# First four weight units of a decoder block loaded and multiplied in pairs, with the value banks moved to the other PSUM pool

## The chip, the cores and the metric

The kernel runs on one NeuronCore of one Trainium2 chip. The metric is the device time of one execution in microseconds (us), smaller is better. Before the change the median of three runs is 462.68 us, between 462.61 and 462.75.

## What is computed

One decoder block over 256 positions of width 1024, all in float32. A wide input projection feeds two token mixers: a gated unit over chunks of 128 positions, and attention in which an indexer picks 64 keys for each query. Both are gated, summed and projected, then come a layer norm, a feed-forward part with a causal convolution of width 3, and a second layer norm.

```python
proj = h @ w_in[i]
u, v, q, k, vv, q_idx, k_idx, w_idx, g_a, g_b = jnp.split(proj, SPLIT_POINTS, axis=-1)
...
mix = jax.nn.sigmoid(g_a) * (a_out @ w_branch_a[i]) + jax.nn.sigmoid(g_b) * (b_out @ w_branch_b[i])
y = mix @ w_o[i]
h = layer_norm(ALPHA * h + y, ln1_g[i], ln1_b[i])
...
f = (jax.nn.silu(gate) * val) @ w_down[i]
h = layer_norm(ALPHA * h + f, ln2_g[i], ln2_b[i])
```

The change touches only the first product, `vv`: the attention values, x (256 x 1024) times a 1024 x 1024 slice of `w_in`.

## The kernel before

All weights but a few small ones are laid out by the host as a row of units of 128 x 2048 floats (1024 KB each), in the order in which they are used. Each unit goes through three steps. SyncE (SP) fetches it into a `raw` buffer, of which there are three (`RB = 3`). ScalarE (ACT) rounds it into `hi` (L77), VectorE (DVE) computes the rest into `lo` (L78). A product of two float32 matrices is then made of three matmuls: x-high by w-high, x-low by w-high and x-high by w-low. There are five `hi` and five `lo` buffers. A `raw` buffer may be filled again when both the cast and the subtraction that read it are done.

`take()` hands out the next unit and asks by `prefetch` (L86 to L98) for units up to four ahead. The loads stand in one SP queue, in order: a load that waits for its buffer holds up all loads behind it.

The value product comes first. Its weights are units 0 to 3: units 0 and 1 hold contraction blocks 0 to 3 for output columns 0 to 511 and 512 to 1023, units 2 and 3 hold blocks 4 to 7 for the same two halves of the columns. Within a unit, columns k*512 to k*512+511 belong to one contraction block. x comes transposed, as eight blocks `xt_sb[:, k]` of 128 x 256 (128 KB each), and is split into `xh` and `xl`.

Before the change unit 0 is fetched in four quarters of 256 KB, each followed by one block of x (L152 with L139 and L128), then unit 1 in two halves, then x blocks 4 to 7 in one load (L154), then unit 2 in two halves. Unit 3 comes whole from `prefetch` (L90). The loop L232 to L243 multiplies unit by unit, 24 matmuls of 128 x 512 for each: four blocks by three products by two position tiles `t`. The sums stand in four PSUM banks that are two tiles of pool A (`bankA`, two buffers of two banks each, L230). The ACT copies of L243 take the first column half out after unit 2 and the second after unit 3. The next product, `qi0` (units 4 and 5, `fm_unit`, L183), takes its bank from pool A too, which by then holds both value tiles. Pool B has four single banks.

In the names that the order of the program prints, `raw0` to `raw7`, `hi0`, `lo0` and so on carry the number of the unit, and `vv0` to `vv3` are the value tiles. What follows a last underscore only counts allocations.

Of the kernel before, what the change touches and what calls it, by code (L numbers as in the profile page):

```python
# [9 lines left out]
F32 = mybir.dt.float32  # L10
F32R = mybir.dt.float32r
AF = mybir.ActivationFunctionType
ALU = mybir.AluOpType
AX = mybir.AxisListType

P = 128
# [10 lines left out]
UN = 2048  # L27
# [13 lines left out]
def kernel(  # L41
# [12 lines left out]
    nc = tc.nc  # L54
# [3 lines left out]
    rawp = ctx.enter_context(tc.tile_pool(name="rawp", bufs=RB))  # L58
    hip = ctx.enter_context(tc.tile_pool(name="hip", bufs=HB))
    lop = ctx.enter_context(tc.tile_pool(name="lop", bufs=LB))  # L60
# [5 lines left out]
    def slot(tag, shape, dt=F32, name=None):  # L66
        return slots.tile(shape, dt, tag=tag, name=name or tag)

    def bankA(shape, name):
        return psA.tile(shape, F32, tag="A", name=name)  # L70

    def bankB(shape, name):
        return psB.tile(shape, F32, tag="B", name=name)

    def split(hi, lo, src, scale=None):
        if scale is None:
            a = nc.scalar.copy(hi, src)  # L77
            return a, nc.vector.tensor_tensor(out=lo, in0=src, in1=hi.bitcast(F32), op=ALU.subtract)  # L78
        else:
            nc.scalar.mul(hi, src, scale)  # L80
            nc.vector.scalar_tensor_tensor(lo, src, scale, hi.bitcast(F32), op0=ALU.mult, op1=ALU.subtract)

    units = {}
    state = {"next": 0}

    def prefetch(upto):  # L86
        while state["next"] <= min(upto, wst.shape[0] - 1):
            i = state["next"]
            raw = rawp.tile([P, UN], F32, tag="raw", name=f"raw{i}")
            nc.sync.dma_start(out=raw, in_=wst[i])  # L90
            hi = hip.tile([P, UN], F32R, tag="hi", name=f"hi{i}")
            lo = lop.tile([P, UN], F32R, tag="lo", name=f"lo{i}")
            n = 4 if i < 4 else 2
            for c in range(n):
                cs = slice(c * UN // n, (c + 1) * UN // n)
                split(hi[:, cs], lo[:, cs], raw[:, cs])
            units[i] = (hi, lo)
            state["next"] += 1  # L98
# [3 lines left out]
    def take(ahead=AHEAD):  # L102
        i = cur["i"]
        cur["i"] += 1
        prefetch(i + ahead)
        return units[i]
# [16 lines left out]
    xt_sb = slot("b2", [P, 2, KC, L], name="xt_sb")[:, 0]  # L123
    x2 = slot("x2", [P, 2, KC, L], F32R, name="x2")
    xh, xl = x2[:, 0], x2[:, 1]

    def load_x(a, b):
        nc.sync.dma_start(out=xt_sb[:, a:b], in_=xt[:, a:b])  # L128

    def load_unit(pieces, pre=None):  # L130
        i = state["next"]
        state["next"] += 1
        raw = rawp.tile([P, UN], F32, tag="raw", name=f"raw{i}")
        hi = hip.tile([P, UN], F32R, tag="hi", name=f"hi{i}")
        lo = lop.tile([P, UN], F32R, tag="lo", name=f"lo{i}")
        n = UN // pieces
        for c in range(pieces):
            cs = slice(c * n, (c + 1) * n)
            nc.sync.dma_start(out=raw[:, cs], in_=wst[i][:, cs])  # L139
            if pre:  # L140
                pre(c)
                with tc.issue_after(prev.ins) if c else nullcontext():
                    nc.vector.tensor_copy(xh[:, c:c + 1], xt_sb[:, c:c + 1])  # L143
                nc.vector.tensor_tensor(out=xl[:, c:c + 1], in0=xt_sb[:, c:c + 1], in1=xh[:, c:c + 1].bitcast(F32),
                                        op=ALU.subtract)
            m = max(1, n // 512)
            for d in range(m):
                ds_ = slice(c * n + d * n // m, c * n + (d + 1) * n // m)
                prev = split(hi[:, ds_], lo[:, ds_], raw[:, ds_])[1]
        units[i] = (hi, lo)  # L150

    load_unit(4, lambda c: load_x(c, c + 1))  # L152
    load_unit(2)
    load_x(4, 8)  # L154
    split(xh[:, 4:8], xl[:, 4:8], xt_sb[:, 4:8])
    load_unit(2)

    ident = const.tile([P, P], F32, name="ident")
    make_identity(nc, ident)
# [23 lines left out]
    def fm_unit(name, m2, hook=None):  # L183
        hi, lo = take()
        bank = bankA([P, 2, 2, L], name)
        fm_chunks(hi, lo, m2, bank, hook)
        return bank

    def fold(bank, dst=None, name="fold"):
        if dst is None:  # L190
            dst = work.tile([P, 2, L], F32, tag="w", name=name)
        nc.scalar.copy(dst, bank[:, :, 1, :])  # L192
        nc.vector.tensor_tensor(out=dst, in0=bank[:, :, 0, :], in1=dst, op=ALU.add)  # L193
        return dst
# [32 lines left out]
            nc.vector.tensor_tensor(out=qs[b, hs, :], in0=bank[a], in1=qs[a, hs, :].bitcast(F32), op=ALU.subtract)  # L227

    vv = a2a[:, 0].rearrange("p (t d) -> p t d", d=D)
    vpair = [bankA([P, 2, 512], f"vv{t}") for t in range(2)]  # L230
    vbanks = [vpair[i // 2][:, i % 2] for i in range(4)]
    for kh in range(2):  # L232
        for hf in range(2):
            hi, lo = take()
            for k in range(4):
                for n, (a, b) in enumerate(((xh, hi), (xl, hi), (xh, lo))):
                    kk = 4 * kh + k
                    for t in range(2):
                        nc.tensor.matmul(vbanks[2 * t + hf], a[:, kk, t * P:(t + 1) * P], b[:, k * 512:k * 512 + 512],  # L239
                                         start=kk == 0 and n == 0, stop=kk == KC - 1 and n == 2)  # L240
            if kh == 1:
                for t in range(2):
                    nc.scalar.copy(vv[:, t, hf * 512:(hf + 1) * 512], vbanks[2 * t + hf])  # L243

    wkb = slot("k", [P, 2, KC, 72], F32R, name="wkb")
    wkh = wkb[:, 0]
# [6 lines left out]
    for u in range(2):  # L253
        b = fold(fm_unit(f"qi{u}", x2), name=f"qif{u}")
# [64 lines left out]
    for u in range(4):  # L319
        b = fm_unit(f"q{u}", x2, {0: kidx_norm, 2: kidx_transpose}.get(u))  # L320
# [6 lines left out]
    for u in range(4):  # L327
        b = fm_unit(f"k{u}", x2)
# [48 lines left out]
    for g, dst in ((0, ga), (1, gb)):  # L377
        for u in range(4):
            i = 4 * g + u
# [4 lines left out]
            b = fm_unit(f"g{g}{u}", x2)  # L384
# [58 lines left out]
    for u in range(4):  # L443
        b = fold(fm_unit(f"u{u}", x2), name=f"uf{u}")
# [7 lines left out]
    for u in range(4):  # L452
        b = fold(fm_unit(f"wb{u}", b2), name=f"wbf{u}")
# [7 lines left out]
    for u in range(4):  # L461
        b = fold(fm_unit(f"wa{u}", a2), name=f"waf{u}")
# [169 lines left out]
    for t in range(2):  # L632
# [25 lines left out]
        for c0, eng in ((512, nc.scalar), (768, nc.sync)):  # L658
            cs = slice(c0, c0 + 256)
# [72 lines left out]
```

## Time and profile before

| | |
|---|---|
| median of three runs | 462.68 us |
| the profiled execution | 463.17 us |
| its span in the profile | 461.5 us |
| TensorE (PE) busy | 450.4 us, 98% of the span |
| DVE, ACT busy | 353.2 us (77%), 258.9 us (56%) |
| moved by DMA | 86.83 MB, 188 GB/s in the mean |

The profile shows one execution. Times within it are counted from the start of the span, and 1.7 us of the execution lie outside of the span. A busy matmul includes its time in the pipeline (about 0.39 us for a 128 x 512 one), so the pace of the engine is read from the distance between starts. A row of a timeline merges neighbouring instructions of one kind; in brackets stands how long the engine idled before it and what ended the wait.

### The profile page before, as it was taken

What the parts mean: (1) busy time and instruction counts of PE and PEld (TensorE: products, weight loads), DVE (VectorE), ACT (ScalarE), POOL (GpSimd) and SP (SyncE); (2) the same over time, 40 slices, a digit from 0 to 9 for tenths busy, and PEclk for the clock granted to TensorE, in tenths of its full rate; (3) what the DMA queues carried; (4) which work ended last, traced back from release to release, by engine and by line L of the source; (5) the groups of instructions that cost most, each with busy time, mean ns of one, the idle gap of its engine ahead of it and who ended that gap; (6) DMA issues with size and microseconds to landing.
All of it is one profiled execution on the core that took longest, in us unless ns stands there. A gap on an engine that the chain in (4) does not pass through costs nothing.

```text
span 461.5 us, 6329 instructions
## 1 busy us (share of the span) xinstructions
PE 450.4 (98%) x2470; PEld 385.4 (84%) x2470; DVE 353.2 (77%) x582; ACT 258.9 (56%) x381; POOL 8.2 (2%) x19
## 2 busy tenths in 40 slices
PE   7999999999999999999999999999999999999993
PEld 3778888888888888898888899888888888888883
DVE  4768878977776559688686869999878677777746
ACT  3678645456474548555454238977655655655600
POOL 0000002000000100001000000000000000000000
PEclk9999999999999999999999999999999999999998
DMA  7978646445344644547746128655654554552002
GB/s 233 381 272 309 260 181 227 178 188 182 104 171 141 254 167 168 190 178 250 297 182 223 51 92 287 241 197 188 240 216 171 194 183 183 182 183 91 2 0 91
DMA packets 14989, 86.83 MB, mean 188 GB/s; under 512 B 1648, under 2 KB 2928, under 8 KB 5744
## 3 DMA queue, kind: packets, MB, share of 16 engines
q1 hardware_dynamic: 13536, 81.98, 48.5%
q0 software_dynamic: 1136, 4.19, 2.7%
q8 instruction: 19, 0.31, 0.3%
q10 hardware_dynamic: 288, 0.26, 0.2%
q14 instruction: 10, 0.08, 0.0%
HBM read 85.39 MB, written 1.05 MB: 187 GB/s over the span
## 4 chain that ended last, share of the span: by engine, by line
PE 95%; DMA 1%; DVE 1%; SPq 1%; ACT 0%; issue 0%; DVEq 0%; ACTq 0%
PE up L171 16%; PE up L170 8%; PE g L171 6%; PE dn L110 4%; PE dn L111 4%; PE dn L109 4%; PE vv L239 4%; PE g L170 3%; PE k L171 3%; PE u L171 3%; PE q L171 3%; PE wb L171 3%; PE wa L171 3%; PE wa L170 2%; PE wb L170 2%; PE q L170 2%
## 5 line engine op out<-in xcount | busy, mean ns | idle before, releaser
L78 DVE TENSOR_TENSOR lo<-raw,hi 128x1024 fp32r<-128x1024 f32 (+1 forms) x158 | 181.0, 1164 | 20.1 <-ACT hi L77 20.0
L77 ACT CAST hi<-raw 128x1024 fp32r<-128x1024 f32 (+1 forms) x158 | 154.5, 1007 | 30.5 <-PE dn L111 12.7
L171 PE MATMUL up<-h,hi 128*128 128x512 f32 x320 | 113.2, 398 | 0.0
L170 PE MATMUL up<-h,lo 128*128 128x256 f32 x320 | 90.0, 281 | 0.0
L171 PEld LDWEIGHTS up<-h,hi 128*128 128x128 f32 x320 | 60.1, 188 | 14.6
L170 PEld LDWEIGHTS up<-h,lo 128*128 128x128 f32 x320 | 60.4, 189 | 0.3
L171 PE MATMUL g<-x,hi 128*128 128x512 f32 x128 | 45.0, 393 | 0.0
L170 PE MATMUL g<-x,lo 128*128 128x256 f32 x128 | 36.5, 286 | 0.0
L193 DVE TENSOR_TENSOR upf<-up,upf 128x512 f32<-128x512 f32 x20 | 13.8, 690 | 19.6 <-ACT upf L192 19.6
L171 PEld LDWEIGHTS g<-x,hi 128*128 128x128 f32 x128 | 24.0, 187 | 5.2
L192 ACT COPY upf<-up 128x512 f32<-128x512 f32 x20 | 11.7, 584 | 27.5 <-PE up L171 27.5
L170 PEld LDWEIGHTS g<-x,lo 128*128 128x128 f32 x128 | 24.2, 189 | 0.0
L532 ACT ACTIVATE y<-upf,cv_sb 128x256 f32<-128x256 f32 x40 | 21.9, 595 | 2.8 <-DVE upf L193 2.8
L171 PE MATMUL u<-x,hi 128*128 128x512 f32 x64 | 22.7, 399 | 0.0
L171 PE MATMUL k<-x,hi 128*128 128x512 f32 x64 | 22.7, 399 | 0.0
L171 PE MATMUL q<-x,hi 128*128 128x512 f32 x64 | 22.5, 393 | 0.0
L171 PE MATMUL wb<-b,hi 128*128 128x512 f32 x64 | 22.3, 391 | 0.0
L171 PE MATMUL wa<-a,hi 128*128 128x512 f32 x64 | 22.2, 391 | 0.0
L239 PE MATMUL vv<-hi,x 128*128 128x512 f32 x64 | 18.6, 402 | 2.2 <-DVE x L143 0.7
L533 DVE SCALAR_TENSOR_TENSOR y<-upf,cv_sb,y 128x255 f32<-128x255 f32 x40 | 17.7, 479 | 0.7 <-ACT y L532 0.7
L170 PE MATMUL wb<-b,lo 128*128 128x256 f32 x64 | 18.2, 284 | 0.0
L170 PE MATMUL q<-x,lo 128*128 128x256 f32 x64 | 18.1, 282 | 0.0
(222 smaller groups left out, 888.1 us busy)
## 6 DMA issues: line engine op xcount, KB each, us to landing
raw<-in_wst_dram SPq DMA_DIRECT2D x72, 1024.0 KB, 4.9
raw<-in_wst_dram SPq DMA_DIRECT2D x4, 512.0 KB, 8.9
raw<-in_wst_dram SPq DMA_DIRECT2D x4, 256.0 KB, 4.3
a2a<-in_par_dram POOLq DMA_DIRECT2D x2, 512.0 KB, 4.7
l1p<-in_par_dram POOLq DMA_DIRECT2D x2, 512.0 KB, 8.5
hres<-in_x_dram POOLq DMA_DIRECT2D x1, 1024.0 KB, 5.1
xt_sb<-in_xt_dram SPq DMA_DIRECT2D x4, 128.0 KB, 4.2
xt_sb<-in_xt_dram SPq DMA_DIRECT2D x1, 512.0 KB, 9.1
```

Of the source, the lines that this page charges most:

```text
L77: a = nc.scalar.copy(hi, src)
L78: return a, nc.vector.tensor_tensor(out=lo, in0=src, in1=hi.bitcast(F32), op=ALU.subtract)
L109: nc.tensor.matmul(ps, ah, bh, start=start, stop=False)
L110: nc.tensor.matmul(ps, ah, bl, start=False, stop=False)
L111: nc.tensor.matmul(ps, al, bh, start=False, stop=stop)
L170: nc.tensor.matmul(ps[:, 0, :], wl, m2k[:, 0], start=start, stop=False, skip_group_check=True)
L171: nc.tensor.matmul(ps, wh, m2k, start=False, stop=stop, skip_group_check=True)
L192: nc.scalar.copy(dst, bank[:, :, 1, :])
L193: nc.vector.tensor_tensor(out=dst, in0=bank[:, :, 0, :], in1=dst, op=ALU.add)
L239: nc.tensor.matmul(vbanks[2 * t + hf], a[:, kk, t * P:(t + 1) * P], b[:, k * 512:k * 512 + 512], start=kk == 0 and n == 0, stop=kk == KC - ...
L532: nc.scalar.activation(y[:, c, :], b[:, c, :], AF.Identity, scale=cv_sb[:, 2, ch:ch + 1], bias=cv_sb[:, 3, ch:ch + 1])
L533: nc.vector.scalar_tensor_tensor(y[:, c, 1:], b[:, c, :L - 1], cv_sb[:, 1, ch:ch + 1], y[:, c, 1:], op0=ALU.mult, op1=ALU.add)
```

## The change

The first four units are loaded as two pairs by a new `load_units`. For units 0 and 1 each of four steps fetches one block of x, then the quarter of unit 0 and the quarter of unit 1 that go with it. For units 2 and 3 each of two steps fetches two blocks of x and a half of each unit. The splits of x are all on DVE now, and the splits of the weights are made to stand behind them. The value loop goes by contraction blocks over both units of a pair (12 matmuls for a block), keeps its four sums in the single banks of pool B, and copies all four out at its end.

```diff
+    def split_x(a, b, after=None):
+        with tc.issue_after(after.ins) if after else nullcontext():
+            nc.vector.tensor_copy(xh[:, a:b], xt_sb[:, a:b])
+        return nc.vector.tensor_tensor(out=xl[:, a:b], in0=xt_sb[:, a:b], in1=xh[:, a:b].bitcast(F32), op=ALU.subtract)
+
+    def load_units(x0, pieces):
+        pair = []
+        for i in (state["next"], state["next"] + 1):
...
+            units[i] = (hi, lo)
+            pair.append((i, raw, hi, lo))
+        state["next"] += 2
+        n, xn = UN // pieces, 4 // pieces
+        prev = None
         for c in range(pieces):
...
+            load_x(x0 + c * xn, x0 + (c + 1) * xn)
+            for i, raw, hi, lo in pair:
+                cs = slice(c * n, (c + 1) * n)
+                nc.sync.dma_start(out=raw[:, cs], in_=wst[i][:, cs])
+            xs = split_x(x0 + c * xn, x0 + (c + 1) * xn, prev)
+            with tc.issue_after(xs.ins):
+                for d in range(n // 512):
+                    for i, raw, hi, lo in pair:
+                        ds_ = slice(c * n + d * 512, c * n + (d + 1) * 512)
+                        prev = split(hi[:, ds_], lo[:, ds_], raw[:, ds_])[1]
+
+    load_units(0, 4)
+    load_units(4, 2)
...
-    vpair = [bankA([P, 2, 512], f"vv{t}") for t in range(2)]
-    vbanks = [vpair[i // 2][:, i % 2] for i in range(4)]
+    vbanks = [bankB([P, 512], f"vv{i}") for i in range(4)]
     for kh in range(2):
...
+        pair = [take() for _ in range(2)]
+        for k in range(4):
+            kk = 4 * kh + k
+            for n, (a, part) in enumerate(((xh, 0), (xl, 0), (xh, 1))):
+                for hf in range(2):
                     for t in range(2):
...
+                        nc.tensor.matmul(vbanks[2 * hf + t], a[:, kk, t * P:(t + 1) * P], pair[hf][part][:, k * 512:k * 512 + 512],
                                          start=kk == 0 and n == 0, stop=kk == KC - 1 and n == 2)
...
+    for hf in range(2):
+        for t in range(2):
+            nc.scalar.copy(vv[:, t, hf * 512:(hf + 1) * 512], vbanks[2 * hf + t])
```

The queue of loads on SP, from the fourth quarter of unit 0 to the load of unit 4, stands before the change as

```order
L139 DMA raw0_93<-in_wst_dram 128x512
L128 DMA xt_sb_91<-in_xt_dram 128x256
L139 DMA raw1_120<-in_wst_dram 128x1024 x2
L128 DMA xt_sb_91<-in_xt_dram 128x1024
L139 DMA raw2_136<-in_wst_dram 128x1024 x2
L90 DMA raw3_161<-in_wst_dram 128x2048
L90 DMA raw4_173<-in_wst_dram 128x2048
```

and from the third quarters of units 0 and 1 to the load of unit 4 after it as

```order
L150 DMA raw0_93<-in_wst_dram 128x512
L150 DMA raw1_96<-in_wst_dram 128x512
L128 DMA xt_sb_91<-in_xt_dram 128x256
L150 DMA raw0_93<-in_wst_dram 128x512
L150 DMA raw1_96<-in_wst_dram 128x512
L128 DMA xt_sb_91<-in_xt_dram 128x512
L150 DMA raw2_135<-in_wst_dram 128x1024
L128 DMA xt_sb_91<-in_xt_dram 128x512
L150 DMA raw3_138<-in_wst_dram 128x1024
L150 DMA raw2_135<-in_wst_dram 128x1024
L150 DMA raw3_138<-in_wst_dram 128x1024
L90 DMA raw4_181<-in_wst_dram 128x2048
```

Units 0 and 1 now arrive together, quarter by quarter. The first load of unit 3, which fills the buffer of unit 0, stands ahead of the second half of unit 2 and of unit 4.

On PE the first contraction block of the value product stands before the change as the first rows of

```order
L239 MATMUL vv0_159<-hi0_94,x2_92 128x512
L239 MATMUL vv1_160<-hi0_94,x2_92 128x512
L239 MATMUL vv0_159<-hi0_94,x2_92 128x512
L239 MATMUL vv1_160<-hi0_94,x2_92 128x512
L239 MATMUL vv0_159<-lo0_95,x2_92 128x512
L239 MATMUL vv1_160<-lo0_95,x2_92 128x512
```

and after it as

```order
L241 MATMUL vv0_177<-hi0_94,x2_92 128x512
L241 MATMUL vv1_178<-hi0_94,x2_92 128x512
L241 MATMUL vv0_177<-hi0_94,x2_92 128x512
L241 MATMUL vv2_179<-hi1_97,x2_92 128x512
L241 MATMUL vv3_180<-hi1_97,x2_92 128x512
L241 MATMUL vv1_178<-hi0_94,x2_92 128x512
L241 MATMUL vv2_179<-hi1_97,x2_92 128x512
L241 MATMUL vv3_180<-hi1_97,x2_92 128x512
L241 MATMUL vv0_177<-lo0_95,x2_92 128x512
L241 MATMUL vv1_178<-lo0_95,x2_92 128x512
L241 MATMUL vv2_179<-lo1_98,x2_92 128x512
L241 MATMUL vv3_180<-lo1_98,x2_92 128x512
```

A block has 12 matmuls in place of 6, and needs a quarter of two units in place of one.

On DVE the work of the first two blocks stands after the change as

```order
L132 CAST x2_92<-xt_sb_91 128x256
L133 TENSOR_TENSOR x2_92<-xt_sb_91,x2_92 128x256
L78 TENSOR_TENSOR lo0_95<-raw0_93,hi0_94 128x512
L78 TENSOR_TENSOR lo1_98<-raw1_96,hi1_97 128x512
L132 CAST x2_92<-xt_sb_91 128x256
L133 TENSOR_TENSOR x2_92<-xt_sb_91,x2_92 128x256
L78 TENSOR_TENSOR lo0_95<-raw0_93,hi0_94 128x512
```

Before it a block had one subtraction of weights (`lo0`); now a block has two, and the split of the next block of x stands behind both.

## Rows read from the trace of the kernel before

**Rows 1.** Page, first part: busy time of each engine.
```profile
PE 450.4 (98%) x2470; PEld 385.4 (84%) x2470; DVE 353.2 (77%) x582; ACT 258.9 (56%) x381; POOL 8.2 (2%) x19
```

**Rows 2.** Windows: stretch, length, busy time by engine, PE clock, DMA share, GB/s.
```profile
31.00:61.00 30.00, 30.00 (x175) 25.95 (x176) 25.11 (x41) 21.51 (x29) 0.00 (x0) 1.00 0.80 300
...
271.00:301.00 30.00, 29.71 (x195) 26.93 (x195) 26.35 (x37) 25.71 (x35) 0.00 (x0) 1.00 0.58 211
...
421.00:451.00 30.00, 30.00 (x152) 25.41 (x151) 18.48 (x32) 10.39 (x15) 0.00 (x0) 1.00 0.01 3
```

**Rows 3.** Chain that ended last, 0 to 80 us: start, length, what.
```profile
4.08 6.69 DMA xt_sb<-in_xt_dram
...
24.63 5.54 PE vv L239 x23
```

**Rows 4.** Timeline of PE, value product and start of qi0: start, length, instructions.
```profile
4.98 1.24 PE L239 MATMUL vv<-hi,x 128*128 128x512 f32 x4 [0.56 <-ACT hi L77]
...
14.50 1.07 PE L239 MATMUL vv<-hi,x 128*128 128x512 f32 x4
...
22.66 1.07 PE L239 MATMUL vv<-hi,x 128*128 128x512 f32 x4
...
30.83 0.38 PE L170 MATMUL qi<-x,lo 128*128 128x256 f32 x1 [0.45 <-ACT a2a L243]
```

**Rows 5.** Waits of PE, 5 to 31 us: total, times, longest.
```profile
PE vv L239 <- ACT a2a L243: 0.5, 1, 0.5
PE qi L170 <- ACT a2a L243: 0.5, 1, 0.5
```

**Rows 6.** Timeline of ACT, casts that a landing released.
```profile
4.25 0.62 ACT L77 CAST hi<-raw 128x512 fp32r<-128x512 f32 x1 [2.16 <-DMA raw<-in_wst_dram]
5.48 0.62 ACT L77 CAST hi<-raw 128x512 fp32r<-128x512 f32 x1 [0.62 <-DMA raw<-in_wst_dram]
7.60 0.62 ACT L77 CAST hi<-raw 128x512 fp32r<-128x512 f32 x1 [1.50 <-DMA raw<-in_wst_dram]
9.85 0.62 ACT L77 CAST hi<-raw 128x512 fp32r<-128x512 f32 x1 [1.63 <-DMA raw<-in_wst_dram]
12.05 2.41 ACT L77 CAST hi<-raw 128x512 fp32r<-128x512 f32 x4 [1.58 <-DMA raw<-in_wst_dram]
...
15.88 2.41 ACT L77 CAST hi<-raw 128x512 fp32r<-128x512 f32 x4 [0.23 <-DMA raw<-in_wst_dram]
```

**Rows 7.** Timeline of DVE: the split of an x block, the subtractions of unit 0.
```profile
4.54 0.29 DVE L143 CAST x<-xt_sb 128x256 fp32r<-128x256 f32 x1 [4.54 <-DMA xt_sb<-in_xt_dram]
4.87 0.43 DVE L144 TENSOR_TENSOR x<-xt_sb,x 128x256 fp32r<-128x256 f32 x1
5.21 0.69 DVE L78 TENSOR_TENSOR lo<-raw,hi 128x512 fp32r<-128x512 f32 x1
...
11.00 0.68 DVE L78 TENSOR_TENSOR lo<-raw,hi 128x512 fp32r<-128x512 f32 x1
```

**Rows 8.** Timeline of SP's queue: first load, load of unit 3.
```profile
0.81 0.38 SPq L139 DMA_DIRECT2D raw<-in_wst_dram  x1
...
11.71 0.33 SPq L90 DMA_DIRECT2D raw<-in_wst_dram  x1
```

**Rows 9.** Waits of SP's queue, 0 to 35 us: total, times, longest.
```profile
SPq L90 <- DVE lo L78: 14.9, 5, 5.2
```

**Rows 10.** Windows of the loading stage, columns as in rows 2.
```profile
7.00:9.00 2.00, 1.94 (x7) 0.97 (x6) 1.20 (x4) 0.62 (x1) 0.00 (x0) 1.00 0.67 191
...
13.00:15.00 2.00, 2.00 (x11) 1.62 (x10) 2.00 (x4) 1.74 (x4) 0.00 (x0) 1.00 1.05 432
```

**Rows 11.** Page, DMA issues: KB each, median us from issue to landing.
```profile
raw<-in_wst_dram SPq DMA_DIRECT2D x72, 1024.0 KB, 4.9
...
raw<-in_wst_dram SPq DMA_DIRECT2D x4, 256.0 KB, 4.3
```

More of the change, by code (lines that the diff above doesn't have):

```diff
@@ L128, in load_x @@
         nc.sync.dma_start(out=xt_sb[:, a:b], in_=xt[:, a:b])
[L130 to L136, printed above, removed]
-        for c in range(pieces):
[L138 to L156, printed above, removed]
+    def split_x(a, b, after=None):
[5 more added lines that the diff above has]
+        for i in (state["next"], state["next"] + 1):
+            raw = rawp.tile([P, UN], F32, tag="raw", name=f"raw{i}")
+            hi = hip.tile([P, UN], F32R, tag="hi", name=f"hi{i}")
+            lo = lop.tile([P, UN], F32R, tag="lo", name=f"lo{i}")
+            units[i] = (hi, lo)
[3 more added lines that the diff above has]
+        prev = None
+        for c in range(pieces):
+            load_x(x0 + c * xn, x0 + (c + 1) * xn)
[8 more added lines that the diff above has]
+                        prev = split(hi[:, ds_], lo[:, ds_], raw[:, ds_])[1]
@@ L229 @@
     vv = a2a[:, 0].rearrange("p (t d) -> p t d", d=D)
-    vpair = [bankA([P, 2, 512], f"vv{t}") for t in range(2)]
-    vbanks = [vpair[i // 2][:, i % 2] for i in range(4)]
+    vbanks = [bankB([P, 512], f"vv{i}") for i in range(4)]
     for kh in range(2):
[L233 to L237, printed above, removed]
+        pair = [take() for _ in range(2)]
[3 more added lines that the diff above has]
+                for hf in range(2):
                     for t in range(2):
-                        nc.tensor.matmul(vbanks[2 * t + hf], a[:, kk, t * P:(t + 1) * P], b[:, k * 512:k * 512 + 512],
+                        nc.tensor.matmul(vbanks[2 * hf + t], a[:, kk, t * P:(t + 1) * P], pair[hf][part][:, k * 512:k * 512 + 512],
                                          start=kk == 0 and n == 0, stop=kk == KC - 1 and n == 2)
-            if kh == 1:
-                for t in range(2):
-                    nc.scalar.copy(vv[:, t, hf * 512:(hf + 1) * 512], vbanks[2 * t + hf])
+    for hf in range(2):
+        for t in range(2):
+            nc.scalar.copy(vv[:, t, hf * 512:(hf + 1) * 512], vbanks[2 * hf + t])
     wkb = slot("k", [P, 2, KC, 72], F32R, name="wkb")
```

## The prediction

> **What bounds the kernel now.** I read the busy shares first: PE is at work for 450.4 of 461.5 us [rows 1]. The windows then show where the rest lies. From 31 to 451 us PE is busy throughout: of 14 stretches of 30 us one shows 29.71, the others at least 29.99 [rows 2], where the first, that one and the last stand. What the change can give or take therefore shows at one point, the start of `qi0` at 30.83 us [rows 4]; whatever moves this start moves the end by as much, so long as later units still come in time.
>
> Next the timeline of PE up to this point. In steady flow six value matmuls start every 1.36 us: the rows at 14.50 and 22.66 are six such groups apart, 8.16 us for 36 matmuls, so 0.227 us each [rows 4]. All 96 need 21.8 us. They take 25.85 (4.98 to 30.83), so PE loses 4.1 us, in three places:
>
> - The group that starts at 22.66 should end at 24.02, and the next unit starts at 24.63 [rows 3, 4]: 0.6 us. Unit 3 writes the second halves of the same PSUM tiles whose first halves are being copied out; the wait is on that copy [rows 5].
> - Unit 3's 24 matmuls need 5.44 us from 24.63, and `qi0` starts 6.20 later: 0.8 us, on the last copies, since both tiles of pool A are taken [rows 5].
> - The other 2.7 us lie before 12 us. There the chain is a load of x [rows 3]: PE eats a block in 1.36 us, and a block plus its quarter (384 KB) comes every 2.2 us (casts released at 5.48, 7.60, 9.85) [rows 6].
>
> **What the change does to each.** *Banks.* The four sums get tiles of their own, and pool A is free for `qi0`. Both bank waits go: 1.4 us. The copies now stand on ACT behind the casts of units 4 and 5, which costs nothing as far as I can see: the next user of these banks comes some 11 us of matmuls later.
>
> *Pairs.* A block now brings 640 KB for 12 matmuls (2.72 us) in place of 384 KB for 6 (1.36 us). Bytes per matmul fall from 64 to 53 KB. When the bytes have come in order, the old rows tell: 256 KB were there at 4.25, 384 at 4.54, 640 at 5.48, 1024 at 7.60, 1408 at 9.85, 2048 at 12.05, 3584 at 15.88 [rows 6, 7]. I lay the new order on this curve. The x block and the quarter of unit 0 (384 KB) are there at 4.54, and after a cast of 0.62 and the 0.11 that a matmul starts behind it (4.25 + 0.62 to 4.98) PE begins at 5.3, against 4.98. Unit 1's quarter comes 0.94 later and costs about half a microsecond. Block 0 ends at 8.4. Block 1 waits for 1280 KB (9.1, cast until 9.8) and ends at 12.1; block 2 needs 1920 KB (11.6) and ends at 14.7; block 3 ends at 17.5. Half of the product is then done, and the other half would end at 28.4, if its data were there: 2.4 us earlier than now.
>
> *The third buffer.* They are not all there. `raw` has three buffers, and unit 3 takes that of unit 0. Before, unit 0 was finished alone, at 11.68, and unit 3 was issued at 11.71 [rows 7, 8]; it was needed after 72 matmuls. Now unit 0 is finished with block 3 only, and unit 3 is needed in block 4, after 50. SP does wait for this release before the change too: five waits on DVE's `lo`, 14.9 us in all [rows 9]. When is unit 0 released? DVE goes through a block as split of x (0.29 and 0.43), `lo` of unit 0, `lo` of unit 1 (0.69 each) [rows 7], in order. For block 2 `lo` of unit 1 follows 1920 KB at 11.6 plus a cast of 0.62, so 13.0; then block 3's split and `lo` of unit 0, 1.41: 14.4. So the first half of unit 3 is issued at about 14.45. No row has 512 KB alone from an idle queue. Below stand 256 KB, 3.4 us from issue to cast (0.81 to 4.25) [rows 6, 8]; above a whole unit, median 4.9 [rows 11]. I take 4.1, the middle, and keep both ends. It lands at 18.55, is cast at 19.17, and PE, which had done two matmuls of block 4 by 17.95, stands for 1.3 us until 19.3. The other 46 matmuls take 10.4: `qi0` starts at 29.7, not 30.83.
>
> The second half of unit 2 is queued behind the waiting load. It is needed after 22 further matmuls, at 24.3, and follows the half of unit 3 by about 1.3 us at the rate of full flow (432 GB/s) [rows 10], so it lands near 20. Unit 4 follows at about 24 and is needed at 29.7. Units 5 to 7 shift by up to 3 us with some 2 us to spare. I cost these at nothing; if unit 5 slips, `qi1` waits.
>
> For the fixed part of a load, the Trainium skill (DMA: Bandwidth & Descriptors, Anatomy of one DMA) fits about 2.0 us plus bytes at 436 GB/s on another issuing path. By that 512 KB would take an estimated 3.2 us in place of my 4.1 and `qi0` would start 0.9 us earlier; the 256 KB row, at 3.4 against 2.6 by the fit, says that the fit is short here.
>
> *Sum.* `qi0` at 29.7 against 30.83: 1.1 us off. On the profiled execution 463.17 becomes 462.1; this execution lies 0.49 above the median of the runs, so on the median I forecast 462.68 - 1.1 = **461.6 us**. The same in other terms: 1.4 from the banks and 2.7 from the starving go; back come 0.3 of later start, 1.3 for the third buffer and 1.4 that remain of waiting in the first three blocks.
>
> **Bounds.** The unknown terms are the pace of the small loads and the landing of unit 3. From 256 KB at 4.25 to 1408 KB at 9.85 the old kernel took in 211 GB/s, and full flow is 432 [rows 6, 10].
>
> **Rivals.**
>
> - *Small loads run faster.* If the slow pace belongs to the first microseconds alone, or to the many short loads of x, which are now a smaller share, quarters may come at 350 GB/s or more. PE then starts at 5.3 and waits 0.5 only; unit 0 is released at about 12, and unit 3 lands by 16.1, in time. `qi0` starts at 5.3 + 0.5 + 21.8 = 27.6: 3.2 off, 459.5 us. For it speaks that the rate was 432 as soon as the pieces were larger. Against it, 191 GB/s were moved from 7 to 9 us, with much already issued [rows 10].
> - *The third buffer takes the gain back.* With unit 3 landing after 4.9 us in place of 4.1, `qi0` starts at 30.5: 0.3 off, 462.4, which no measurement can tell from no change. A measurement of this kernel tells about 0.2%, 0.93 us.
> - *Slower: the small pace stays for all twelve pieces, and unit 3 pays for it.* At 211 GB/s the last quarter of unit 0 (2304 KB) comes at 14.2, `lo` is done at 15.7, and unit 3, with 4.9 us to land, is there at 20.6. PE waits until 21.3, `qi0` starts at 31.8, 0.9 to 1.0 later: 463.6. It decides at a landing of 19.7: behind this the kernel is slower. The Trainium skill speaks for this one (DMA: Bandwidth & Descriptors, Bandwidth): loads should be batched to a mebibyte or more. The change goes the other way, from eight short loads at the start to twelve, and no run here yet shows the pace of such a longer row.
>
> **How the numbers follow.** I give the forecast 0.43, the fast pace 0.20, the gain taken back 0.27, the slow one 0.10. The forecast lies only 0.2 us beyond what can be told, so a fifth of its chance goes to no change. Faster by over 0.2%: 0.34 + 0.20 = 0.54; same: 0.09 + 0.27 = 0.36; slower: 0.10. The range reaches from near the fast case to short of the slow one's worst: 459.7 to 463.4. The likeliest value is 461.6.
>
> **What would show it.** In the profile after, the waits of PE on the copies of `vv` ahead of `qi0` are gone. `qi0` starts at 29.7. SP issues the first half of unit 3 near 14.4, released by DVE's `lo`, and PE waits once for more than a microsecond early in block 4, for ACT's cast of unit 3. From then on PE is without gaps as before. I am wrong if that issue comes at 12 or 16, if unit 3's half lands outside 17.8 to 19.4, or if a gap shows behind `qi0`, at `qi1` or `kwb`, because units 5 or 6 slipped.

## The result and the profile after

| | median | from | to | executions |
|---|---|---|---|---|
| before | 462.86 us | 462.21 | 463.76 | 12 |
| after | 465.17 us | 463.62 | 468.13 | 12 |

The ratio is 1.0054, with a 95% interval of 1.0037 to 1.0072. The kernel became slower by half a per cent; forecast were 461.6 us and a range of 459.7 to 463.4. The profiled execution, 463.62 us, is the fastest of the twelve, so its profile shows the change at its best.

The page of the kernel after, busy shares and DMA issues [rows 1, 11]:

```profile
PE 450.5 (98%) x2470; PEld 387.2 (84%) x2470; DVE 354.0 (77%) x585; ACT 258.0 (56%) x380; POOL 8.2 (2%) x19
...
raw<-in_wst_dram SPq DMA_DIRECT2D x8, 256.0 KB, 6.2
raw<-in_wst_dram SPq DMA_DIRECT2D x4, 512.0 KB, 5.1
```

The busy shares are those of before. The windows of the kernel after [rows 2, 10]:

```profile
7.00:9.00 2.00, 2.00 (x6) 1.61 (x5) 0.51 (x2) 0.33 (x1) 0.00 (x0) 1.00 1.01 359
...
31.00:61.00 30.00, 28.36 (x165) 24.21 (x164) 26.75 (x43) 23.61 (x33) 0.00 (x0) 1.00 0.79 297
```

Before, PE was busy throughout from 31 to 61 us. Now 1.64 us are missing there. The timeline of PE after [rows 4] shows what was won and where it went:

```profile
5.53 3.71 PE L241 MATMUL vv<-hi,x 128*128 128x512 f32 x8 [1.12 <-ACT hi L77]
...
10.00 1.98 PE L241 MATMUL vv<-hi,x 128*128 128x512 f32 x8
...
18.17 2.02 PE L241 MATMUL vv<-hi,x 128*128 128x512 f32 x8
...
29.11 0.28 PE L173 MATMUL qi<-x,lo 128*128 128x256 f32 x1
...
49.59 0.32 PE L269 MATMUL kwp<-ident,a2a 72*128 72x72 f32 x2 [1.64 <-DVE a2a L263]
```

`qi0` starts 1.7 us earlier, at 29.11 in place of 30.83. The two transposes `kwp` then stand at 49.59, after a wait; without it they would follow the matmul at 47.55 by 0.23. They read the folded product `kwb` (L262, L263). This product is made of x and of `wk`, a small load of its own, and comes behind `qi1` on PE. (`fm_unit` takes one unit: `qi0` is the product of unit 4 alone, not of units 4 and 5, and `qi1` that of unit 5.) Units 6 to 9 stand before its fold only through the order of work on ACT and DVE: the matmuls of `kwb` ended at 43.4, and its copy (L262) came up on ACT at 46.98, behind the casts of units 8 and 9. The waits of PE up to 70 us [rows 5]; the waits on the copies of `vv` are gone:

```profile
PE kwp L269 <- DVE a2a L263: 1.6, 1, 1.6
PE vv L241 <- ACT hi L77: 1.1, 1, 1.1
```

In the trace of before the subtractions of unit 2, the same fold and `kwp` stand so:

```profile
16.82 2.49 DVE L78 TENSOR_TENSOR lo<-raw,hi 128x512 fp32r<-128x512 f32 x4
...
48.08 0.42 DVE L261 TENSOR_TENSOR a2a<-kwb,a2a 72x256 f32<-72x256 f32 x1
...
49.06 0.29 PE L267 MATMUL kwp<-ident,a2a 72*128 72x72 f32 x2
```

The fold ended at 48.50, and PE came to `kwp` at 49.06: the room was 0.56 us, not 2. After the change PE comes at 47.78 (1.28 earlier, one pair of matmuls of the lead having moved ahead of `kwp` in PE's order) and the fold ends at 49.46 (0.96 later). Less the room that makes 1.68; `kwp` starts 0.13 behind the fold, and the sum is the 1.81 us from 47.78 to 49.59, of which the profile counts 1.64 as idle. The chain that ended last, kernel after [rows 3], tells why the fold is late:

```profile
13.87 3.88 DMA raw<-in_wst_dram
17.77 0.63 ACT hi L77
...
21.30 0.69 DVE lo L78
22.01 7.37 DMA raw<-in_wst_dram
29.49 2.00 ACT hi L77 x2
31.48 0.43 ACT a2a L245
...
32.34 0.60 ACT a2a L245
32.94 0.96 ACT hi L77
...
39.33 0.61 DVE qif L196
39.97 0.62 ACT qs L229
...
41.25 1.06 ACT hi L77
...
49.03 0.43 DVE a2a L263
49.59 0.32 PE kwp L269 x2
```

Read from the top: the first half of unit 3 is issued at 13.87, when the buffer of unit 0 is free, and lands 3.88 later. The second half of unit 2 stands behind it in SP's queue and lands at 18.98, 1.9 later than before; on DVE it then stands behind the first half of unit 3 and a split of x. So unit 2 is subtracted (`lo`, 21.30) late; its buffer goes to unit 5, asked for at 22.01 in place of 19.34 and cast at 29.49. (This load took 7.4 us in both traces.) The copies of `vv` (`a2a` L245) and the cast of unit 6 follow that cast on ACT, and each next step stands behind the last, down to the fold. Before, the subtractions of unit 2 ended at 19.31, and the casts of units 4 and 5 ran in one row on ACT from 24.95:

```profile
24.95 3.93 ACT L77 CAST hi<-raw 128x1024 fp32r<-128x1024 f32 x4
...
31.15 2.02 ACT L77 CAST hi<-raw 128x1024 fp32r<-128x1024 f32 x2
...
40.31 2.00 ACT L77 CAST hi<-raw 128x1024 fp32r<-128x1024 f32 x2
```

Unit 6 was cast at 31.15 (32.82 after) and unit 8 at 40.31 (41.25 after). SP's waits after [rows 9] name the hold itself:

```profile
SPq L90 <- DVE lo L78: 6.9, 3, 3.2
...
SPq L150 <- DVE lo L78: 1.8, 1, 1.8
```

### The profile page after: what moved, and what is told of

Its sections match the earlier page's. It is cut to its first block, busy times and chain, and to the rows that moved or that the text cites. A ratio compares the mean times of both kernels' runs of the same rounds, so it can differ in the third digit from the quotient of the medians.

```text
span 461.9 us, 6337 instructions
## 1 busy us (share of the span) xinstructions
PE 450.5 (98%) x2470; PEld 387.2 (84%) x2470; DVE 354.0 (77%) x585; ACT 258.0 (56%) x380; POOL 8.2 (2%) x19
## 4 chain that ended last, share of the span: by engine, by line
PE 87%; DVE 4%; DMA 4%; ACT 2%; issue 1%; SPq 1%; DVEq 0%; ACTq 0%
PE up L174 16%; PE up L173 8%; PE g L174 6%; PE dn L110 4%; PE dn L111 4%; PE dn L109 4%; DMA raw<-in_wst_dram 4%; PE g L173 3%; PE u L174 3%; PE k L174 3%; PE wb L174 3%; PE wa L174 3%; DVE lo L78 3%; PE q L174 3%; PE wa L173 2%; PE wb L173 2%
## 5 line engine op out<-in xcount | busy, mean ns | idle before, releaser
L241 PE MATMUL vv<-hi,x 128*128 128x512 f32 x64 | 17.6, 421 | 1.1 <-ACT hi L77 1.1
```

Of the source, the lines that this page charges most:

```text
L241: nc.tensor.matmul(vbanks[2 * hf + t], a[:, kk, t * P:(t + 1) * P], pair[hf][part][:, k * 512:k * 512 + 512], start=kk == 0 and n == 0, st ...
```

## The experiments

"Traced" is the profiled execution. `qi0` is its start, "rest" the span less that start: what everything behind the value product took. "Wait" is what PE stood at `kwp` or `kT2ps` (the transposes of the indexer keys, later on), "clock" the granted clock from 46 to 61 us where it was not full. Ratios are to runs of the kernel before on the same chip.

| kernel | median (n) | ratio, interval | `qi0` | wait | clock | rest |
|---|---|---|---|---|---|---|
| before | 462.86 (12) | | 30.83 | none | | 430.7 |
| after | 465.17 (12) | 1.0054, 1.0037 to 1.0072 | 29.11 | 1.6 | | 432.8 |
| same_again | 467.77 (1) | | 29.61 | 3.8 | 0.89 | 436.5 |
| late_hook | 466.88 (9) | 1.0076, 1.0053 to 1.0098 | 29.32 | 0.4 + 2.7 | 0.72 (60 to 66) | 436.4 |
| warm11 | 466.44 (7) | 1.0046, 1.0008 to 1.0084 | 29.19 | 3.9 | 0.77 | 437.4 |
| banks_only | 462.37 (10) | 0.9970, 0.9958 to 0.9982 | 29.47 | 0.2 | | 430.7 |
| banks_again | 462.13 (10) | 0.9972, 0.9962 to 0.9983 | 29.23 | 0.2 | | 430.8 |
| first_pair | 462.35 (10) | 0.9967, 0.9945 to 0.9988 | 29.68 | none | | 431.0 |
| own_buffer | 461.83 (10) | 0.9961, 0.9943 to 0.9980 | 28.45 | 2.2 | 0.89 | 434.5 |
| own_again | 462.25 (12) | 0.9972, 0.9961 to 0.9983 | 28.66 | 1.2 | | 432.4 |
| unit2_first | 462.72 (12) | 0.9985, 0.9973 to 0.9997 | 29.07 | 1.5 | | 432.7 |
| u8_late | 463.02 (10) | 0.9984, 0.9967 to 1.0000 | 28.71 | 0.7 | | 431.9 |
| own_u8_late | 462.70 (10) | 0.9970, 0.9950 to 0.9990 | 29.50 | 0.8 | | 431.9 |
| banks_u8_late | 462.67 (10) | 0.9982, 0.9967 to 0.9997 | 29.36 | 0.7 | | 431.2 |
| own_two | 461.91 (6) | 0.9965, 0.9952 to 0.9979 | 29.54 | none | | 430.6 |

The last column is the study in short. Where PE waits by 0.2 us or less behind `qi0`, the rest takes 430.6 to 431.0 us, whatever the loads look like. Where it waits longer, the rest grows by the wait and by what the clock loses (read from the distance between starts: 1.4 us in same_again and own_buffer, 1.7 in late_hook, 2.7 in warm11), to within a microsecond.

**The kernel after once more** (unchanged, one execution).

> The changed kernel once more, nothing edited. Chain theory (what was gained before qi0 is lost in one wait of PE at the transposes kwp near 48 us, because the casts and subtractions of units 5 to 7 come later): again 463.6 us, within 0.3. Clock theory (in most executions PE's clock is at its lower level for some microseconds of the first 30 us, and that makes the spread from 463.6 to 468.1): a time above 464, a mean granted clock below 0.996, and in the trace value matmuls that start 0.43 us apart, in place of 0.227, in a stretch outside of that seen in the first profile (5.5 to 9.1 us).

Measured 467.77. The waits of PE, the windows, and on ACT the cast of unit 8:

```profile
PE kwp L269 <- DVE a2a L263: 3.8, 1, 3.8
```

```profile
46.00:61.00 15.00, 11.17 (x58) 9.47 (x57) 12.84 (x25) 10.53 (x15) 0.00 (x0) 0.89 0.70 258
```

```profile
43.94 2.00 ACT L77 CAST hi<-raw 128x1024 fp32r<-128x1024 f32 x2 [2.24 <-DMA raw<-in_wst_dram]
```

A slower execution of the same kernel waits 2.2 us longer at the same place, since unit 8 lands late: it took 7.1 us from its issue, 4.8 in the first trace. From the end of the wait on the granted clock is lower: from `kwp` to the sixth matmul of `q` with `lo` PE takes 3.30 us, 1.94 in the first trace, so 1.4 us are lost. Against before: 1.2 won at `qi0`, 5.8 lost behind it. The clock theory of the expectation, a slow stretch in the first 30 us, is not what made this execution long; the clock fell at 51.8. The other eleven executions of the kernel after were not traced, but their mean granted clocks fit the same picture: the six above 465 us show 0.990 to 0.993, five of the six below it 0.995 to 0.998 (463.81 has 0.991).

**`kwp` later in PE's order.**

```diff
...
-        b = fm_unit(f"q{u}", x2, {0: kidx_norm, 2: kidx_transpose}.get(u))
+        b = fm_unit(f"q{u}", x2, {1: kidx_norm, 2: kidx_transpose}.get(u), (0, 3) if u == 1 else (0, 5))
```

> The changed kernel with the transposes kwp put 12 matmuls later in PE's order (from the first product q0 into q1). Chain theory: the wait of 1.6 to 1.9 us at kwp goes, and no other takes its place; the median falls by about 1.7, to 463.5 from 465.2, and an execution with the clock of the first profile takes 461.9. Clock theory alone: the spread of some 4 us stays, and the median stays within 0.5 of 465.2. Both: median near 463.5 with the spread.

The waits of PE in late_hook:

```profile
PE kT2ps L287 <- DVE a2a L282: 2.7, 2, 2.1
...
PE kwp L269 <- DVE a2a L263: 0.4, 1, 0.4
```

On ACT, the cast of unit 9:

```profile
45.18 2.00 ACT L77 CAST hi<-raw 128x1024 fp32r<-128x1024 f32 x2 [2.57 <-DMA raw<-in_wst_dram]
```

It failed, 466.88: the transposes moved back by 12 matmuls only, and the next user of the same chain, `kT2ps`, then waits 2.7. The lateness is in the data, not in the place of the instruction that reads it. Its source in this execution is another: unit 5 landed 5.2 us after its issue, and units 5 to 8 were cast as early as before (27.15, 30.48, 34.09, 40.13). Unit 9 took 7.5 us and was cast 2.5 us later than before (42.72).

**A longer warm-up of PE** (`WARM = 8` becomes 11).

> The changed kernel with 11 warm-up matmuls in place of 8, so that PE is at work until about 5.7 us and no gap lies ahead of the first value matmul at 5.5. Clock theory: value matmuls start 0.227 us apart from their first on, the mean granted clock is 0.997 in every execution, and the spread goes: all times between 463.2 and 464.0, since the wait at kwp stays and takes what the front gains. Chain theory alone, with the spread from elsewhere (the loads): median near 465.2 with times up to 468.

The wait of PE behind the product in warm11:

```profile
PE kwp L269 <- DVE a2a L263: 3.9, 1, 3.9
```

466.44, still slower than before. The value product's waits fell to 0.5 us, and the wait at `kwp` was 3.9, with unit 8 landing 7.1 us after its issue. The slow first block of the product is not the cause of the loss.

**The banks alone** (to the kernel before).

```diff
-    vpair = [bankA([P, 2, 512], f"vv{t}") for t in range(2)]
-    vbanks = [vpair[i // 2][:, i % 2] for i in range(4)]
+    vbanks = [bankB([P, 512], f"vv{i}") for i in range(4)]
```

> The kernel before with one part of the change: the value sums in four single banks of pool B; loads and order of the matmuls as before. qi0 starts about 1.4 us earlier, at 29.4. Chain theory: before the change kwp had only 0.5 us of room (its input was written at 48.5, PE came at 49.06), and that input comes at the same time, so PE waits there for about 0.9 and the kernel gains 0.5: 462.3. Rival (nothing waits behind qi0, as the prediction had it): the whole 1.4, 461.4.

The only wait of PE behind `qi0` in banks_only, and the fold on DVE:

```profile
PE kT2ps L284 <- DVE a2a L279: 0.2, 1, 0.2
```

```profile
47.06 0.42 DVE L260 TENSOR_TENSOR a2a<-kwb,a2a 72x256 f32<-72x256 f32 x1
```

0.3% faster: `qi0` at 29.47, 1.36 earlier, and all of it kept, as the rival had it; the chain theory, with a wait of 0.9, missed. The copies of `vv` ran earlier too (29.44 in place of 30.19), so the cast of unit 6 behind them and the fold came 1.0 earlier, and PE found no wait at `kwp`. (In this kernel's order 15 pairs of `q` matmuls stand ahead of `kwp`, 12 before; even at the place of before PE would have come at 47.70, behind the fold.) This part of the change is a gain by itself; the loss is in the loads.

**A buffer of its own for unit 3** (the second half of the slot that `xt_sb` lies in is unused then).

```diff
...
-            raw = rawp.tile([P, UN], F32, tag="raw", name=f"raw{i}")
+            if i == 3:
+                raw = xt2[:, 1].rearrange("p k l -> p (k l)")
+            else:
+                raw = rawp.tile([P, UN], F32, tag="raw", name=f"raw{i}")
```

> The changed kernel with one thing taken away: unit 3 is fetched into the unused half of the tile that holds transposed x, so that it doesn't wait for the buffer of unit 0. Buffer theory (the wait of SP's queue for unit 0 holds back unit 2's second half, so unit 5, then units 6 to 8, whose casts stand ahead of the folds of qi0, qi1 and kwb on ACT): unit 5 lands by 25 in place of 29.5, the input of kwp is written by 47.5 in place of 49.4 to 52.1, PE waits there for less than 0.5, its clock does not fall near 51; median 1.5 to 2 below the kernel before (461.5 to 462), spread under 1.5 us. Rival (the pairs themselves, by the longer row of short loads or the copies of vv behind the casts of units 4 and 5, make the chain late): the wait at kwp stays above 1.5 and the median stays 2 above the kernel before.

461.83, faster than before by 0.39%, the time that the buffer theory gave. Unit 2 is no longer held in SP's queue, and unit 5 is cast at 26.97 in place of 29.49. The profiled execution is the slowest of its ten, 464.59, and does not show the theory's other steps: unit 8 landed late there (7.3 us), PE waited 2.2 at `kwp` and the clock fell. The other nine lie between 460.61 and 462.35; none of them was traced.

**The first pair alone.** Units 0 and 1 in pairs as in the change; x blocks 4 to 7, unit 2 and unit 3 loaded as before, and multiplied unit by unit:

```diff
-    load_units(4, 2)
...
+    load_x(4, 8)
...
+    state["next"] = 3
...
-        for k in range(4):
+        for hs, k in [((0, 1), k) for k in range(4)] if kh == 0 else [((hf,), k) for hf in range(2) for k in range(4)]:
```

> The changed kernel with the second pair undone: units 0 and 1 in pairs, x blocks 4 to 7 in one load, unit 2 in two halves, unit 3 whole from the prefetch, and the second half of the product unit by unit, all in pool B. Unit 3 still takes the buffer of unit 0, but no load of unit 2 stands behind that wait, and PE needs unit 3 only after 72 matmuls. Buffer theory: unit 2 is done by 18, unit 5 issued by 19 in place of 22 and landed by 26.5; the wait at kwp is under 0.7; median 462 to 463. Rival (units 0 and 1 being released together is enough to hold up units 4 to 8): the wait at kwp stays above 1.5, the clock falls behind it, median above 464.5.

462.35, 0.33% faster, and no wait behind `qi0` (one of the ten took 465.75, with a mean granted clock of 0.989; the others end at 462.54). So it is the second pair that costs: it asks for unit 3 at a time when its buffer is not free, and puts half of unit 2 behind it.

**Unit 8 out of the way.** The cast and subtraction of unit 8 are made to stand behind the fold of `kwb` on ACT and DVE (`issue_after`, and the `qi` units look two units ahead). Unit 9, which stood between unit 8 and the fold, goes behind it too. This is done in the kernel after, in the one with a buffer of its own for unit 3, and with the banks alone.

> The changed kernel with the cast and subtraction of unit 8 put behind the fold of kwb in ACT's and DVE's order (and its load asked for two products later), nothing else. Order theory (ACT and DVE work in order; the late unit 8 stands ahead of the folds of qi1 and kwb, so its landing decides when kwp can run): the input of kwp is written by 46 whatever unit 8 does, PE does not wait at kwp, the clock does not fall near 51, and the gain of 1.7 at qi0 reaches the end but for a wait of up to 1 at kT2ps, behind units 9 and 10: median 462 to 463.5. Rival (the lateness comes from units 6 and 7 and the copies of vv alone): a wait at kwp above 1 stays, median above 464.5.

> Both: unit 3 in the unused half of the tile of transposed x, and unit 8 behind the fold of kwb. Both theories: no wait of PE above 0.5 between the first block and 60 us, the clock stays up, qi0 at 28.5 to 29.1, spread under 1.5; median 460.8 to 461.6, 2 to 2.5 below the kernel before. Rival (unit 8's place matters only where the buffers are late): the same as own_buffer, 461.8.

> The kernel before with the value sums in pool B and unit 8 behind the fold of kwb, loads and matmuls unpaired. Order theory: nothing waited there for unit 8 in banks_only (it landed 0.5 before its turn), so the same median within 0.3: 462.1 to 462.6. Rival (the fold order is itself worth something): below 461.8.

463.02, 462.70 and 462.67; own_u8_late missed its theory (no wait above 0.5, 460.8 to 461.6) and is by its ratio level with own_buffer, as the rival had it. In u8_late the fold ended at 44.05 though unit 8 took 7.3 us, and the wait is no longer at `kwp`:

```profile
PE kT2ps L290 <- DVE a2a L285: 0.7, 1, 0.7
```

The kernel after gains 0.7% from this edit (1.0054 to 0.9984), and its executions lie within 1.3 us in place of 4.5: the order on ACT and DVE behind late units is what carries the loss to PE. The banks alone do not gain by it (0.9982 against 0.9970): there unit 8 was in time. The three end level, at a new wait of 0.7 to 0.8.

**Unit 2 first.** Three buffers and pairs as in the change, but both halves of unit 2 are loaded, cast and subtracted ahead of unit 3, and x blocks 4 to 7 come in one load.

> Three raw buffers and products by pairs as in the change; only the second half of unit 2, and its casts and subtractions, stand ahead of those of unit 3, and blocks 4 to 7 of x come in one load. Theory (a load that waits for a buffer holds unit 2's second half, and with it the buffer of unit 2, unit 5 and all casts behind): SP issues that half near 10 us in place of 13.9, unit 2 is subtracted by about 18 in place of 22.0, unit 5 is issued by 17 in place of 22 and cast by 27, qi0 stays near 29, and PE does not wait at kwp by more than 0.5. Time 461.3 to 462.5, 0.2 to 0.5% faster than before. Rival (loading in pairs with three buffers is late as such, since unit 3 takes the buffer of unit 0): nothing is won by the order, PE waits 1.5 to 4 at kwp, 464 to 467.

The chain of unit2_first:

```profile
13.60 5.12 DMA raw<-in_wst_dram
...
33.52 7.51 DMA raw<-in_wst_dram
...
41.11 1.06 ACT hi L77
...
49.45 0.32 PE kwp L286 x2
```

462.72, 0.15% faster: the loss is gone with the order of the second pair's loads, casts and subtractions (and x in one load), with the same three buffers. Unit 5 is cast at 26.34, as expected. But the wait at `kwp` stays 1.5, not under 0.5: now unit 8 (issued 33.52) takes 7.51 us and is cast at 41.11 only.

**The two best on one chip.**

> The pairs with a buffer of its own for unit 3 once more, beside the two others on one chip: 461.5 to 462.3, faster than before by 0.3 to 0.5%. Theory (with the casts back in time the shorter start counts): ahead of the banks alone by 0.1 to 0.2%. Rival (the start does not matter, only the banks do): level with the banks alone.

> The old loads with the four value tiles in pool B once more, beside the two others on one chip: 0.3% faster than before, 462.0 to 462.8. Theory: 0.1 to 0.2% behind the pairs with a freed buffer. Rival (only the banks matter): level with them.

0.9972 both: level. The rival has it, though for another reason than it gave. `qi0` starts 0.6 earlier with the pairs (28.66 against 29.23), and the chain of own_again shows where that goes:

```profile
28.18 0.89 ACT a2a L249 x2
...
29.75 0.95 ACT hi L77
...
33.11 7.14 DMA raw<-in_wst_dram
...
40.32 1.06 ACT hi L77
...
48.67 0.32 PE kwp L273 x2
```

The copies of `vv` stand ahead of the cast of unit 6, whose buffer goes to unit 8. Unit 8 is asked for 0.5 us earlier than in banks_again all the same (33.11 against 33.64), but takes 7.14 us in place of 4.70, and PE waits 1.2 us at `kwp`.

**Unit 8 fetched early** (own_buffer, with unit 8 in that same buffer, which is free once unit 3 is split).

```diff
...
+            if i == 8:
+                raw = xt2[:, 1].rearrange("p k l -> p (k l)")
...
```

> The pairs with a buffer of its own for unit 3, and unit 8 fetched into that same buffer, free again when unit 3 is split, so that it no longer waits for the buffer of unit 6 and is asked for near 31 us in place of 33.1. Theory (with a buffer of its own for unit 3 the casts of units 5 to 7 are in time, and what is left of the wait at kwp, 1.2 and 2.2 us in the two traces, is unit 8 landing at 40.3 and 41.2): unit 8 is cast by 39, kwp and kT2ps wait less than 0.5 us in sum, and the time is 460.2 to 461.6, 0.4 to 0.7% faster than before and ahead of the pairs with the one buffer by 0.2%. Rival (the late part of a load comes wherever the row of loads is dense, and moves to unit 9): unit 8 is in time but PE waits over 1 us for unit 9 or at kT2ps, 461.8 to 462.6.

Unit 8 is asked for at 30.23 and cast at 37.80; it takes 7.5 us here too, but is in time. The waits of PE from 4 to 90 us are one line:

```profile
PE vv L248 <- ACT hi L77: 1.2, 1, 1.2
```

There is no wait behind `qi0`, and the rest is 430.6 as in before: in this trace unit 3's buffer and unit 8's earlier request together leave nothing behind `qi0` of what held the earlier start back. The time, 461.91 or 0.35% faster, missed the expected gain by a little. In the traced execution `qi0` stood at 29.54, a microsecond behind own_buffer's, behind slow first matmuls (last section); a lead over own_buffer was not resolved. The loss of the change can be removed, and four versions beat both kernels: the banks alone, the first pair alone, and the pairs with one or two loads in the free half of the slot. They can't be told apart.

## Why the prediction was wrong

- *The banks: right.* 1.4 forecast, 1.36 in banks_only, kept to the end.
- *Start and first blocks: near, by other terms.* PE began at 5.53 (forecast 5.3). The bytes came at 359 GB/s from 7 to 9 us, where 191 had been [rows 10]; yet the first eight matmuls took 3.71 us, and 1.98 later, since they ran at the lower clock (last section), a term that the prediction does not have. Block 0 ended at 10.00 (8.4); from there PE stood no more, and block 1 ended at 12.73 (12.1).
- *The third buffer: right in the load, wrong in its effect.* Issue at 13.87 (14.45), 3.88 to the cast (4.1), at 17.77 (18.55 and a cast), just ahead of the 17.8 to 19.4 that it allowed. PE reached block 4 at 18.17 and did not wait: the 1.3 us were not paid there. `qi0` stood at 29.11, 0.6 earlier than forecast. The half of unit 2 behind it landed at 18.98 (near 20) and was in time for PE, as forecast.
- *The step that failed* is "Units 5 to 7 shift by up to 3 us with some 2 us to spare. I cost these at nothing". The shift was there: unit 2's buffer was free for unit 5 at 22.01 in place of 19.31, 2.7 us. The sentence gives no row for its 2 us; it names only `qi1`, a product that reads one of these units itself. But ACT and DVE work in order, and behind the casts of units 5 to 9 stands the fold that `kwp` reads, with 0.56 us of room. The sentence that the copies on ACT cost nothing is in doubt with it: in after and in own_again they are pieces of the chain that ended last, but no run took their price apart. The condition that the prediction gave for being wrong, a gap behind `qi0` because units 5 or 6 slipped, came true, at `kwp` and not at `qi1` or `kwb`.
- *What was not priced at all*: units 8 and 9 landing after 7 us in place of 4.7, and the clock behind a long wait. With its wait of 1.6 us the traced execution stays within 0.2% of before; in same_again, late_hook and warm11, all above 467 us, these two are what is added. That they make up the rest of the median's loss is likely and not shown, for the executions near the median were not traced.
- *The rivals.* The fast one had its pace (359 GB/s in that window, 350 asked for), but unit 0 was free at 13.85 and not near 12, and `qi0` won 1.7 us and not 3.2. The slower one (the small pace stays, unit 3 pays) had the sign and the wrong mechanism: unit 3 was in time and `qi0` early. That it gave 463.6 us, close to the traced 463.62, is chance. The one in which the third buffer takes the gain back failed likewise: the load of unit 3 cost PE nothing.

## What to carry to other kernels

When work is moved forward on the busiest engine, price the helpers in order: for every engine that works its queue in order, list what stands behind a delayed piece, and find the consumer with the least room, not the consumer of the delayed piece. Room is read as the time between the end of the producer and the start of its reader in the trace of before; half a microsecond of it bounds a gain ahead of it wherever the producer does not move along. Ask that too: banks_only kept all of its 1.36 us, since the same edit brought the fold 1.0 earlier. A load that must wait for a buffer belongs behind the loads that need not.

## What the runs showed of the hardware

- *PE's clock after a wait.* Behind waits of 3.8 and 3.9 us (same_again, warm11), 2.7 in two pieces (late_hook) and 2.2 (own_buffer) the granted clock fell to its lower level, 1.2 of 2.4 GHz, for 3.4 us, in warm11 for 6.8; in all but late_hook the fall came within a microsecond before the end of the wait. Behind waits of 1.6, 1.5 and 1.2 at `kwp` (after, unit2_first, own_again) it stayed full. In first_pair it fell at 6.9, behind a wait of 1.6 before the first value matmul, three matmuls and a wait of 0.3. In late_hook the windows around it read:

```profile
60.00:66.00 6.00, 5.56 (x24) 4.76 (x25) 2.98 (x6) 1.00 (x2) 0.00 (x0) 0.72 0.36 131
```

  The Trainium skill (TensorE: Matmul & The Clock Gate, HAM oscillation — how this bites in real kernels) says that a wait for data can throttle PE so that the next piece starts on the slow clock; these rows agree, at a cost of 1.4 us in same_again.

- *One late share of a load.* Unit 8 took 4.7 to 4.8 us in before, banks_only, banks_again, banks_u8_late, first_pair, own_u8_late and the first trace of after, 5.9 in late_hook, and 7.1 to 7.5 in same_again, warm11, own_buffer, own_again, unit2_first, u8_late and own_two. Other loads show the same two lengths: unit 5 took 7.4 in before and after, 5.2 in banks_only, late_hook and u8_late. The sixteen landings of unit 8 tell how: in before the first came at 39.09, the ninth at 39.18, the last at 39.29; in own_again at 37.44, 37.67 and 40.24, the fifteenth at 37.73. One share is 2.5 us behind the other fifteen. The Trainium skill (DMA: Bandwidth & Descriptors, Why a DMA increments its semaphore by 16 and not by 1) says that a transfer counts as landed with the last of its engines; the trace agrees. What holds that share back, and why for unit 8 mostly with the second pair, stays open: no run here took it apart.
- *The first matmuls run at either clock.* The same eight matmuls took from 2.12 us (same_again) to 3.78 (own_two). Where they are slow they start 0.43 us apart, and 0.23 apart from one point on; at a recorded clock of 0.50 the value matmuls of first_pair (7 to 10 us) start 0.43 apart too:

```profile
7.00:8.00 1.00, 1.00 (x3) 0.81 (x4) 0.96 (x3) 0.00 (x0) 0.00 (x0) 0.50 0.78 202
```

  The traces' own clock records begin with a rise to the full level. In after and own_two it comes at that very point, 9.02 and 9.94 us; where it comes at 4.04 (same_again) or 4.80 (own_again), ahead of the value product, no value matmul is slow. Ahead of the first record the clock column shows 1.00 all the same. So the same kernel can stand at the lower level until 4 us in one execution (same_again) and until 9 in another (after). Among the kernels with the same loads at the start, `qi0` stood at 28.45 and 28.66 where the rise came early (own_buffer, own_again) and at 29.50 and 29.54 where it came at 10.20 and 9.94 (own_u8_late, own_two). Why the rise comes early or late was not tried.
